# Making every second weight unit's low part by an accumulating DMA instead of a VectorE difference

## The chip, the cores and the metric

The kernel runs on one core of a Trainium2 chip. The metric is the device time of one execution in microseconds (us); the figure quoted is the median of several runs. The profile is one execution recorded by the hardware profiler.

## The reference, cut to what matters

Two layers of a hybrid backbone with 512 tokens (256 context, 256 latent) and 1024 channels in float32. In each layer a modulated RMS norm feeds one wide input projection; its columns go to three token mixers (a gated linear recurrence, a chunkwise retention with four heads, a latent attention with eight heads). Each mixer's output is gated, multiplied by a 1024x1024 down projection, weighted by a sigmoid merge gate and added; the sum goes through a 1024x1024 output projection and, gated, onto the residual.

```python
z = (m_a * ((ya * silu(ga)) @ w_down_a) + m_b * ((yb * silu(gb)) @ w_down_b)
     + m_c * ((yc * silu(gc)) @ w_down_c))
x = x + gate * (z @ w_out)
```

The second layer's output is wanted for the latent tokens only, so its queries, gates and down projections run on 256 columns, while its keys, values and recurrence inputs run on 512.

## The kernel before, in words

**Split operands.** TensorE works on `float32r` operands, which keep fewer bits than float32. To keep accuracy every operand is split into a high part (the value cast to `float32r`) and a low part (value minus high part, also `float32r`), and each product is three matmuls: high by high, high by low, low by high (`mm3`, line 520). `split` makes the pair: `A.copy(hi, src)` on ScalarE and `V.tensor_tensor(lo, src, f(hi), op=ALU.subtract)` on VectorE.

**Weight units.** The weights are packed into units of 128 partitions by 1024 floats (512 KB). There are 14 kinds of unit, eight of each kind (j = 0 to 7) and two layers: 224 units, fetched by `unit(l, kind, j)`. `load` takes a `raw` buffer, has SP's queue load the unit from HBM into it, takes one `whi` and one `wlo` buffer and splits `raw` into them. There are five buffers each of `raw`, `whi` and `wlo` (`NRAW`, `NHI`, `NLO`). The same `load` serves the smaller weights (`wup`, `wlru`, `wkv`, `wqd` and part of `wmod`), 72 more loads that are split. A unit feeds 24 matmuls of 512 columns, or of 256 columns in most of the second layer; an output unit (`wo`) there feeds twelve of 512.

**Who uses a unit.** `proj` multiplies one unit's eight 128x128 blocks with the normed tokens: inputs of the recurrence (`xa`), of the retention (`q`, `k`; values by `ret_pair`), the gates (`silu_gate`) and the merge gates. `merge` alternates, for j = 0 to 7, a merge gate unit and a down projection unit of the same j. The end of each layer takes the eight `wo` units: the first four for the left half of the columns, the last four, loaded together, for the right half; then come the residual and, in the second layer, the store of the output.

**The order of the work.** Nothing is emitted directly. A `Recorder` notes every operation with its buffers, and `schedule` replays the list in a planner: each operation has a cost from `_cost` (and for a DMA a lag to landing), engines take the earliest recorded operation that is ready and whose output buffer is free, and the resulting order is emitted engine by engine. So every engine runs a fixed order that depends on the planner's prices, and a changed price or operation can move all that comes after it. All recorded operations are emitted by one line, L368 of the profile. SP's price for a load is its bytes by 370 per ns plus 30 ns, with 2000 ns of lag; GpSimd ("POOL") so far does `power` (the norms' inverse square roots) and four small fills.

**Buffers.** A `raw` buffer is free for the next load when the high and low parts of its unit are made; `whi` and `wlo` are free when TensorE has run the unit's last matmul.

Of the kernel before, what the change touches and what calls it, by code (L numbers as in the profile page):

```python
# [12 lines left out]
F32R = mybir.dt.float32r  # L13
AF = mybir.ActivationFunctionType
ALU = mybir.AluOpType
# [30 lines left out]
UNIT = {kind: 8 * i for i, kind in enumerate(UNIT_KINDS)}  # L46
# [342 lines left out]
class Engine:  # L389
# [3 lines left out]
    def __getattr__(self, method):  # L393
        def call(*args, **kwargs):
            views = [x for x in list(args) + list(kwargs.values()) if isinstance(x, View)]
            outs = [x for x in (args[0], kwargs.get("accum_out")) if isinstance(x, View)]
            ins = [v for v in views if all(v is not o for o in outs)]
            cost, lag = _cost(self.name, method, args, kwargs)
            return self.rec.add(self.name, method, args, kwargs, outs, ins, cost, lag)

        return call
# [6 lines left out]
def _size(v):  # L408
    return v.idx.size


def _cost(engine, method, args, kwargs):
    out = args[0]
    n = _size(out) if isinstance(out, View) else 0
    if engine == "PE":
        if method == "transpose":
            return 107.0, 0.0
        passes = 1 if args[1].buf.dtype == F32R else 4
        return max(passes * n / 2.4, 27.0 if passes == 1 else 211.0) + 2.7, 0.0
    if engine == "SP":  # L420
        size = 4 * int(np.prod(args[1].shape))
        return size / 370.0 + 30.0, 2000.0
    psum = any(isinstance(x, View) and x.buf.psum for x in args[1:])
    if engine == "ACT":
        ptr = sum(isinstance(kwargs.get(k), View) for k in ("scale", "bias"))
        return (50.0 if psum else 93.0) + 0.834 * n + 93.0 * (ptr + ("accum_out" in kwargs)), 0.0
    if engine == "POOL":
        if kwargs.get("op") == ALU.pow:
            return 300.0 + 165.0 * n, 0.0
        return 100.0 + 2.2 * n, 0.0  # L430
    ptr = any(isinstance(x, View) for x in args[2:4])
    if method == "tensor_scalar":
        if psum:
            return 186.0 + 1.04 * n, 0.0
        return (129.0 if ptr else 67.0) + 0.523 * n, 0.0
    if method == "scalar_tensor_tensor":
        return 66.0 + (61.0 if isinstance(args[2], View) else 0.0) + 1.047 * n, 0.0
    if method in ("tensor_reduce", "bn_stats"):
        return 66.0 + 1.04 * _size(args[1]), 0.0
    if method == "reciprocal":  # L440
        return 66.0 + 6.3 * n, 0.0
    if method in ("tensor_copy", "memset"):
        return 66.0 + 0.53 * n, 0.0
    return 66.0 + 1.045 * n, 0.0
# [3 lines left out]
def tile_hybrid(ctx, tc, ins, out):  # L448
    nc = tc.nc
    rec = Recorder(nc)  # L450
    T, V, A, G, S = (Engine(rec, e) for e in ("PE", "DVE", "ACT", "POOL", "SP"))
# [51 lines left out]
    def f(ap):  # L503
        return ap.bitcast(F32)

    def split(hi, lo, src):
        A.copy(hi, src)
        V.tensor_tensor(lo, src, f(hi), op=ALU.subtract)
# [18 lines left out]
    def load_raw(src, n=1024):  # L527
        raw = rec.tile("raw", [128, 1024], F32)
        S.dma_start(raw[:, 0:n], src)
        return raw[:, 0:n]  # L530

    def load(src, n=1024):
        raw = load_raw(src, n)
        hi = rec.tile("whi", [128, 1024], F32R)[:, 0:n]
        lo = rec.tile("wlo", [128, 1024], F32R)[:, 0:n]
        split(hi, lo, raw)
        return hi, lo

    def unit(l, kind, j):
        return load(ins["wu"][l, UNIT[kind] + j])  # L540

    ident = ctile([128, 128], name="ident")
    make_identity(nc, ident.buf.tile())
# [136 lines left out]
    def proj(ps, l, kind, j, lat):  # L680
        hh, hl = hcur
        hi, lo = unit(l, kind, j)
        c = slice(256, 512) if lat else slice(0, 512)
        ps = ps[:, 0:256] if lat else ps
        mm3(ps, [(hi[:, k * 128:(k + 1) * 128], lo[:, k * 128:(k + 1) * 128], hh[:, k, c], hl[:, k, c]) for k in range(8)])
        return ps
# [274 lines left out]
    def merge(l, br, zt, first, last):  # L961
        names = {0: ("gmc", "dc"), 1: ("gma", "da"), 2: ("gmb", "db")}[br]
        n = 512 if l == 0 else 256
        slab = Slab()
        ys = ys_out[br]
        for j in range(8):
            pg = proj(bank(), l, names[0], j, l == 1)
            t = small()[:, 0:n]
            A.activation(t, pg, AF.Tanh, scale=0.5)
            yield  # L970
            hi, lo = unit(l, names[1], j)
            pd = bank()[:, 0:n]
            mm3(pd, [(hi[:, k * 128:(k + 1) * 128], lo[:, k * 128:(k + 1) * 128], *ys[k]) for k in range(8)])
            z = zt[j]
            if first:
                V.scalar_tensor_tensor(z, t, 1.0, pd, op0=ALU.add, op1=ALU.mult)
            else:
                V.scalar_tensor_tensor(t, t, 1.0, pd, op0=ALU.add, op1=ALU.mult)
                V.tensor_tensor(z, z, t, op=ALU.add)
            if last:  # L980
                zh, zl = slab.pair(n)
                A.activation(zh, z, AF.Copy, scale=0.5)
                V.scalar_tensor_tensor(zl, z, 0.5, f(zh), op0=ALU.mult, op1=ALU.subtract)
                zs.append((zh, zl))
            yield
# [18 lines left out]
    def ret_pair(l, p):  # L1004
        hh, hl = hcur
        banks = [bank() for _ in range(NTT)]
        for kp in range(4):
            hi, lo = unit(l, "v", 4 * p + kp)
            for tt in range(NTT):
                s = slice(tt * 128, (tt + 1) * 128)  # L1010
                for kk in range(2):
                    k = 2 * kp + kk
                    w = slice(kk * 512, (kk + 1) * 512)
                    mm3(banks[tt], [(hh[:, k, s], hl[:, k, s], hi[:, w], lo[:, w])], start=k == 0, stop=k == 7)
            yield
        vt = []
        for tt in range(NTT):
            vt.append(Slab().pair(512))
            split(*vt[-1], banks[tt])
        for i in range(2):  # L1020
            yield from ret_head(l, 2 * p + i, [(a[:, i * 256:(i + 1) * 256], b[:, i * 256:(i + 1) * 256]) for a, b in vt])
# [164 lines left out]
    for l in range(DEPTH):  # L1186
# [57 lines left out]
        for k2 in range(4):  # L1244
            hi, lo = unit(l, "wo", k2)
# [132 lines left out]
```

## Time and profile before

| what | value |
|---|---|
| device time, median of 3 runs | 1411.13 us (1410.71 to 1414.93) |
| profiled execution, first to last instruction (span) | 1409.4 us; no time of its own beside the span is recorded |
| TensorE (PE) busy | 1392.1 us, 99% |
| VectorE (DVE) busy | 1039.0 us, 74% |
| ScalarE (ACT) busy | 813.1 us, 58% |
| GpSimd (POOL) busy | 86.2 us, 6% |
| mean granted TensorE clock | 0.997 of full speed |
| DMA from HBM | 167.87 MB, 120 GB/s over the span |

"Busy" is the time in which an engine had at least one instruction running; durations of matmuls overlap, so their sum is more than the busy time. The DMA share is the mean busy share of the core's 16 DMA engines. "Landing" is the time from a DMA's issue to the arrival of its data.

### The profile page before, as it was taken

Reading aid. Unit: us, or ns where it says so; the run is one execution under the profiler, and the core shown is the slowest. Engines: PE = TensorE matmul, PEld = TensorE weight load, DVE = VectorE, ACT = ScalarE, POOL = GpSimd, SP = SyncE. Lnnn points to the kernel's source line nnn. Section 1 sums busy time; section 2 is a strip of 40 time slices with the busy share of each in tenths; the row PEclk is TensorE's granted clock in tenths of the full one; section 3 lists DMA queues with packets and bytes.
Section 4 is the critical chain, followed back from the end, with each engine's and each line's share of the span. In section 5 each row is a group of like instructions: output and inputs, shape, how many; then the busy total and the mean of one; then the engine's idle time right before and its main releaser. Section 6 shows DMA issues by size and latency. Waiting matters only on the chain.

```text
span 1409.4 us, 20895 instructions
## 1 busy us (share of the span) xinstructions
PE 1392.1 (99%) x7742; PEld 1211.3 (86%) x7742; DVE 1039.0 (74%) x2059; ACT 813.1 (58%) x1610; POOL 86.2 (6%) x112
## 2 busy tenths in 40 slices
PE   6999999999999999999999999999999999999998
PEld 3888888888888888888888888999898989899997
DVE  7689987667668655574884765899777888888664
ACT  7685664676668323153432226877686777854442
POOL 1031210000000000010000001311000000000000
PEclk9999999999999999999999999999999999999999
DMA  8512212223233423413344451332343444456452
GB/s 317 182 33 92 69 34 80 96 78 111 90 113 120 150 94 100 133 56 112 110 142 137 135 183 60 118 104 83 100 140 112 143 128 145 162 167 209 140 180 76
DMA packets 50990, 170.28 MB, mean 121 GB/s; under 512 B 5956, under 2 KB 7748, under 8 KB 50888
## 3 DMA queue, kind: packets, MB, share of 16 engines
q1 hardware_dynamic: 50888, 168.94, 36.0%
q8 instruction: 61, 1.00, 0.3%
q14 instruction: 41, 0.34, 0.1%
HBM read 167.87 MB, written 1.05 MB: 120 GB/s over the span
## 4 chain that ended last, share of the span: by engine, by line
PE 94%; DVE 3%; DMA 1%; ACT 1%; issue 0%; POOL 0%; SPq 0%; ACTq 0%; DVEq 0%; POOLq 0%
PE mm L368 94%; DVE sm L368 1%; DVE t L368 1%; DMA raw<-in_wmod_dram 1%; DVE wlo L368 1%; DMA t<-in_xin_dram 0%; DVE st L368 0%; POOL st L368 0%; ACT sm L368 0%; SPq L368 0%; ACT whi L368 0%; ACT t L368 0%; ACT hh L368 0%; DVE hl L368 0%; ACTq L368 0%
## 5 line engine op out<-in xcount | busy, mean ns | idle before, releaser
L368 ACT CAST whi<-raw 128x1024 fp32r<-128x1024 f32 (+3 forms) x296 | 292.3, 997 | 356.2 <-PE mm L368 292.0
L368 DVE TENSOR_TENSOR wlo<-raw,whi 128x1024 fp32r<-128x1024 f32 (+3 forms) x296 | 338.1, 1147 | 145.0 <-ACT whi L368 141.9
L368 PE MATMUL mm<-hh,whi 128*128 128x512 f32 (+1 forms) x1152 | 404.3, 351 | 0.0
L368 PE MATMUL mm<-hl,whi 128*128 128x512 f32 (+1 forms) x1152 | 402.6, 350 | 0.0
L368 PE MATMUL mm<-hh,wlo 128*128 128x512 f32 (+1 forms) x1152 | 402.6, 349 | 0.0
L368 PEld LDWEIGHTS mm<-hh,wlo 128*128 128x128 f32 x1152 | 218.0, 189 | 27.0
L368 PEld LDWEIGHTS mm<-hl,whi 128*128 128x128 f32 x1152 | 218.1, 189 | 26.4
L368 PEld LDWEIGHTS mm<-hh,whi 128*128 128x128 f32 x1152 | 218.0, 189 | 26.2
L368 PE MATMUL mm<-t,whi 128*128 128x512 f32 (+1 forms) x896 | 230.1, 344 | 0.0
L368 PEld LDWEIGHTS mm<-t,whi 128*128 128x128 f32 x896 | 156.0, 190 | 19.9
L368 POOL TENSOR_TENSOR st<-st,nhalf 128x2 f32<-128x2 f32 (+2 forms) x102 | 83.6, 826 | 1234.1 <-DVE st L368 1215.7
L368 PE MATMUL mm<-t,t 128*128 128x256 f32 (+1 forms) x912 | 153.6, 310 | 0.5 <-ACT t L368 0.5
L368 PE MATMUL mm<-t,wlo 128*128 128x512 f32 (+1 forms) x448 | 154.1, 344 | 0.0
L368 PE MATMUL mm<-whi,t 128*128 128x512 f32 (+1 forms) x464 | 146.0, 380 | 0.4 <-DVE t L368 0.4
L368 PEld LDWEIGHTS mm<-t,t 128*128 128x128 f32 x912 | 129.0, 190 | 11.0 <-ACT t L368 0.9
L368 ACT ACTIVATE sm<-mm 128x128 f32<-128x128 f32 (+4 forms) x278 | 95.4, 358 | 20.2 <-PE mm L368 17.1
L368 ACT CAST t<-sm 128x256 fp32r<-128x256 f32 (+1 forms) x128 | 60.6, 486 | 71.3 <-DVE sm L368 68.0
L368 PEld LDWEIGHTS mm<-whi,t 128*128 128x128 f32 x464 | 85.7, 188 | 11.7 <-DVE t L368 0.6
L368 PEld LDWEIGHTS mm<-t,wlo 128*128 128x128 f32 x448 | 84.9, 189 | 10.0
L368 PE MATMUL mm<-wlo,t 128*128 128x512 f32 (+1 forms) x232 | 88.0, 379 | 0.0
L368 PE MATMUL mm<-wlo,hh 128*128 128x512 f32 (+2 forms) x240 | 86.6, 363 | 0.0
L368 PE MATMUL mm<-whi,hh 128*128 128x512 f32 (+2 forms) x240 | 86.1, 362 | 0.4 <-ACT whi L368 0.4
(110 smaller groups left out, 1730.4 us busy)
## 6 DMA issues: line engine op xcount, KB each, us to landing
raw<-in_wu_dram SPq DMA_DIRECT2D x224, 512.0 KB, 3.5
raw<-in_wmod_dram SPq DMA_DIRECT2D x48, 512.0 KB, 4.5
t<-in_xin_dram SPq DMA_DIRECT2D x8, 512.0 KB, 7.5
raw<-in_wup_dram SPq DMA_DIRECT2D x8, 512.0 KB, 4.2
raw<-in_wlru_dram SPq DMA_DIRECT2D x16, 256.0 KB, 2.7
raw<-in_wqd_dram SPq DMA_DIRECT2D x8, 384.0 KB, 3.0
raw<-in_wup_dram SPq DMA_DIRECT2D x8, 384.0 KB, 3.1
raw<-in_wkv_dram SPq DMA_DIRECT2D x8, 320.0 KB, 3.9
```

The lines of the kernel that those rows point to most:

```text
L368: getattr(eng[op.engine], op.method)(*[r(x) for x in op.args], **{k: r(v) for k, v in op.kwargs.items()})
```

## The change

The planner gets a price for a DMA issued by GpSimd, and every unit with an odd j goes through a new `load_summed`: the cast into `whi` stays; ScalarE also writes minus the high part into `wlo`; then a DMA issued by GpSimd adds the raw weights onto it, both ends in SBUF.

```diff
     if engine == "POOL":
+        if method == "dma_start":
+            return 1100.0, 4000.0
         if kwargs.get("op") == ALU.pow:
@@
+    def load_summed(src):
+        raw = load_raw(src)
+        hi = rec.tile("whi", [128, 1024], F32R)
+        lo = rec.tile("wlo", [128, 1024], F32R)
+        A.copy(hi, raw)
+        A.activation(lo, f(hi), AF.Copy, scale=-1.0)
+        G.dma_start(lo, raw, accum_op=ALU.add)
+        return hi, lo
+
     def unit(l, kind, j):
-        return load(ins["wu"][l, UNIT[kind] + j])
+        return (load_summed if j % 2 else load)(ins["wu"][l, UNIT[kind] + j])
```

## Rows read from the trace of the kernel before

**Rows 1.** The page's part 1: busy time, share of span and instructions by engine.

```profile
PE 1392.1 (99%) x7742; PEld 1211.3 (86%) x7742; DVE 1039.0 (74%) x2059; ACT 813.1 (58%) x1610; POOL 86.2 (6%) x112
```

**Rows 2.** Windows of 35 us, all engines: busy us (instructions), then TensorE clock, DMA share, GB/s.

```profile
0.00:35.00 35.00, 24.22 (x110) 12.50 (x111) 24.70 (x43) 26.45 (x39) 4.81 (x14) 0.95 0.87 317
35.00:70.00 35.00, 33.97 (x202) 31.10 (x200) 23.76 (x56) 23.98 (x59) 2.76 (x4) 0.95 0.57 186
70.00:105.00 35.00, 34.47 (x196) 30.12 (x195) 28.46 (x94) 29.97 (x120) 12.10 (x16) 1.00 0.11 33
105.00:140.00 35.00, 34.48 (x199) 29.32 (x198) 33.80 (x116) 20.62 (x74) 6.74 (x6) 1.00 0.29 93
245.00:280.00 35.00, 35.00 (x156) 28.96 (x156) 22.84 (x29) 22.38 (x30) 0.00 (x0) 1.00 0.30 97
```

**Rows 3.** The page's part 4: the chain of waits, shares by engine.

```profile
PE 94%; DVE 3%; DMA 1%; ACT 1%; issue 0%; POOL 0%; SPq 0%; ACTq 0%; DVEq 0%; POOLq 0%
```

**Rows 4.** Groups of instructions over the span, costliest first: ScalarE, VectorE, GpSimd.

```profile
L368 ACT CAST whi<-raw 128x1024 fp32r<-128x1024 f32 (+3 forms) x296 | 292.3, 997 | 356.2 <-PE mm L368 292.0 <-issue 42.1 <-DMA raw<-in_wu_dram 13.6
L368 DVE TENSOR_TENSOR wlo<-raw,whi 128x1024 fp32r<-128x1024 f32 (+3 forms) x296 | 338.1, 1147 | 145.0 <-ACT whi L368 141.9
L368 POOL TENSOR_TENSOR st<-st,nhalf 128x2 f32<-128x2 f32 (+2 forms) x102 | 83.6, 826 | 1234.1 <-DVE st L368 1215.7 <-ACT t L368 12.0 <-DVE sm L368 5.4
```

**Rows 5.** Waits over the span, engines and the SP queue: us, times, longest.

```profile
ACT whi L368 <- PE mm L368: 292.0, 137, 4.9
...
SPq L368 <- DVE wlo L368: 923.8, 227, 20.9
```

**Rows 6.** DMA: two issue rows, SP's time per issue (ns), landing times of `raw` (us).

```profile
raw<-in_wu_dram SPq DMA_DIRECT2D x224, 512.0 KB, 3.5
raw<-in_wlru_dram SPq DMA_DIRECT2D x16, 256.0 KB, 2.7
...
L368 SPq DMA_DIRECT2D raw<-in_wu_dram x224: 327/328/328, 63.0 to 1379.7; - x112
DMA to landing us min/median/max: 2.4/3.5/9.3
```

**Rows 7.** Windows by stage of the second layer, all engines, columns as in Rows 2.

```profile
1085.00:1225.00 140.00, 140.00 (x923) 128.92 (x922) 119.59 (x207) 114.91 (x170) 2.62 (x4) 1.00 0.41 134
1225.00:1260.00 35.00, 35.00 (x224) 31.83 (x223) 29.89 (x48) 20.96 (x28) 0.00 (x0) 1.00 0.62 210
...
1330.00:1365.00 35.00, 35.00 (x292) 34.92 (x291) 22.20 (x32) 16.56 (x24) 0.00 (x0) 1.00 0.55 181
1365.00:1386.00 21.00, 21.00 (x165) 20.49 (x165) 13.62 (x20) 9.86 (x14) 0.00 (x0) 1.00 0.46 153
```

**Rows 8.** The same windows, VectorE's differences into `wlo` alone: window length, busy (count), clock, DMA, GB/s.

```profile
1085.00:1225.00 140.00, 42.35 (x38) 1.00 0.41 134
1225.00:1260.00 35.00, 12.59 (x12) 1.00 0.62 210
...
1330.00:1365.00 35.00, 14.66 (x13) 1.00 0.55 181
1365.00:1386.00 21.00, 8.89 (x8) 1.00 0.46 153
```

**Rows 9.** Timeline of the last stage, ScalarE and TensorE: start us, duration us.

```profile
1357.25 1.05 ACT L368 CAST whi<-raw 128x1024 fp32r<-128x1024 f32 x1 [1.40 <-PE mm L368]
1360.13 1.05 ACT L368 CAST whi<-raw 128x1024 fp32r<-128x1024 f32 x1 [1.55 <-issue]
...
1391.48 1.05 ACT L368 CAST whi<-raw 128x1024 fp32r<-128x1024 f32 x1 [1.67 <-PE mm L368]
...
1398.26 0.39 PE L368 MATMUL mm<-wlo,t 128*128 128x512 f32 x1
1404.61 0.39 PE L368 MATMUL mm<-whi,t 128*128 128x512 f32 x1
```

## The prediction, made before the changed kernel ran

> **What bounds the kernel now.** I read the busy times first, then the windows, the chain, the groups with their waits, the DMA and at last the timeline. TensorE is busy for 1392.1 of 1409.4 us, VectorE for 74% and ScalarE for 58% of the span [rows 1]. Of TensorE's 17.3 us of idle time 10.8 lie in the first 35 us and 2.1 between 35 and 140 us; a window in the middle of the first layer shows 35.00 of 35.00 [rows 2]; the rest, 4.4 us, is the span after the last matmul, which ends at 1405.0 us [rows 9]. The chain agrees: 94% of it is matmuls, 3% VectorE [rows 3]. So work taken off VectorE is worth nothing unless TensorE waited for it, and the first load of a unit that could change starts only at 63 us [rows 6]. What can change the time is a low part that comes too late.
>
> How early they come now is seen in the waits: ScalarE's cast waited 292.0 us for TensorE to leave a `whi` buffer, and SP's loads 923.8 us for VectorE to finish with a `raw` buffer [rows 5]. Buffers are kept full; loads run as soon as a buffer is given back.
>
> **The change part by part.** Of each kind's eight units four have an odd j: 14 x 4 x 2 = 112 units.
>
> *VectorE loses* 112 differences of 1.15 us [rows 4], 128 us, from 74% to about 65%. They lay beside matmuls, so this gives 0; at most the 2.1 us of idle TensorE time between 35 and 140 us come back.
>
> *ScalarE gains* 112 copies of 128x1024. I price each as the cast of that size, 1.05 us [rows 9]: 118 us, from 58% to 66%. The tightest stage is 1085 to 1225 us, where it is busy 114.9 of 140 us [rows 7]; 38 split units run there [rows 8], so about 19 copies add 20 us: 134.9 of 140. It still fits: 0, with a rival below.
>
> *GpSimd gains* 112 issues beside 102 powers of 0.83 us [rows 4]. The trace has no DMA of GpSimd. SP's issue takes 0.33 us [rows 6], the planner's new price in the diff is 1.1; I take 1.1, with 0.33 and 2.2 as ends. That makes 123 us on an engine busy for 86. A power queued behind such an issue waits for the copy before it plus 1.1 us; the powers stand mostly where norms are made, with few units about, so 0, at most 1 us.
>
> *The low part comes later.* Before, 1.05 us of cast and 1.15 of difference lay between a free buffer and a finished unit. After, it is cast, copy and X, from the issue of the adding DMA to its landing. Bounds for X from loads: the shortest landing is 2.4 us; the longest, 9.3, plus once more the transfer and 1.1 of issue gives 12.0 [rows 6]. In between, 256 KB land in 2.7 us and 512 KB in 3.5 [rows 6]: 1.6 us per 512 KB moved and 1.9 fixed. The add has two inputs of 512 KB, so I take X = 1.1 + 1.9 + 2 x 1.6 = 6.2 us.
>
> TensorE needs a refilled buffer only after the four other units. Casts of successive units in the last merge stand 2.88 us apart (1357.25, 1360.13) [rows 9], so the lead there is 4 x 2.88 = 11.5 us, against 1.05 + 1.05 + 6.2 = 8.3. Hidden, with 3.2 us left. In the first layer 156 matmuls take 35 us [rows 2], 5.4 us per unit of 24, and the lead is 21.5 us: hidden even at X = 12.0. At that end 2.6 us would be missing in the second layer, once per eight units or so (a stall gives the next units their lead back). On SP, `raw` is held for 8.3 us in place of 2.2, and all loads queue behind the one that waits for it; with 3.5 us for the next load that is 11.8 us, under the five units' 14.4. Hidden too, at this X.
>
> *The end* has no such lead. The last unit's cast starts at 1391.48, when TensorE leaves a buffer, and its low part is first used at 1398.26 [rows 9]. The new chain is ready at 1391.48 + 2.1 + 6.2 = 1399.8: **1.5 us late**, with everything after it. Ends: 0 (X under 4.7) and 5.8 us (X = 12.0).
>
> *The DMA engines gain* 112 transfers. The share of 0.55 at 181 GB/s between 1330 and 1365 us [rows 7] means 0.55 x 0.524 MB / 181 GB/s = 1.59 us of all 16 engines per 512 KB load. For the add I bound the engines' time c by 1.59 us (one move) and 4.8 us (two inputs and one output as three moves) and take two moves, 3.2 us, one per input, the middle of the two. That these transfers use the same 16 engines as the loads no row shows, since all data goes through one queue. I take it so; with engines of their own the terms that follow would be 0 and the sum 1.5 us. The Trainium skill, DMA: Bandwidth & Descriptors, section Issuing engines are not separate DMA queues, says that DMAs of SP, ScalarE and GpSimd end on the same 16 engines and interleave; no run here shows it yet, and by it the terms stand.
>
> Now by stage, loads plus adds [rows 7, 8]. 1085 to 1225 us: 0.41 x 140 + 19 x 3.2 = 118 of 140 us, fits. 1225 to 1260: 0.62 x 35 + 6 x 3.2 = 40.8 of 35, **5.8 us short**. 1330 to 1386: 0.55 x 35 + 0.46 x 21 + 10.5 x 3.2 = 62.3 of 56, **6.3 us short**. The 3.2 us of lead left take up a part of each: 2.6 + 3.1 = 5.7 us of waiting matmuls. The middle of the first layer, 0.30 x 35 + 3.25 x 3.2 = 21 of 35 [rows 2], fits.
>
> **Sum:** 0 + 0 + 0 + 5.7 + 1.5 = 7.2 us on the span of 1409.4, so 1416.6. The runs' median of 1411.13 is 1.7 us above that span, which I carry over: **1418.3 us**, 0.5% slower. About 0.3%, 4.2 us, is what a measurement of this kernel can tell from no change.
>
> **Rival 1, not slower: the add is cheap.** Both inputs lie in SBUF and the loads' rate is one from HBM; nothing says that an SBUF read takes as long. At c = 2.4 the two short stages need 36.1 of 35 and 54.1 of 56 us, which the lead covers, X becomes 5.4 and the end 0.7 us late: 1411.13 + 0.7 = 1411.8. It decides below c = 3.0, where the three terms together fall under 4.2 us. For it: 3.0 is near what I take. Against it: the adding DMA does more per byte than a load. The Trainium skill, DMA: Bandwidth & Descriptors, section Where 436 GB/s comes from, has transfers inside SBUF bound by a fabric of 435 GB/s; two inputs would then take 2.4 us, an estimate from that page, and the sum would be this rival's. No run here shows that rate.
>
> **Rival 2, much slower: the add is heavy.** At three moves, c = 4.8, the stage from 1085 needs 148 of 140, that from 1225 50.5 of 35, the last 79 of 56: 46 us short, less 3.2 in each of the three, and X = 7.8 puts the end 3.1 us late: about 40 us, 1451. For it: the same arithmetic with one move more. Against it: the planner's price of a load, by its formula 3.4 us, is close to the 3.5 that the trace shows [rows 6], and its new price of an add is 5.1 us in all, less than even my X.
>
> **Rival 3, slower by a little: ScalarE's order.** In 1085 to 1225 us 25.1 us are free for 19 copies; above 1.32 us per copy, its own and what its waits add, ScalarE is the bound and casts come late. At some 5 us of lost time: 1416. For it: the chance waits of a full engine. Against it: the lead of 11.5 us and more.
>
> **Faster** would need TensorE's idle time; 2.1 us are to be had, 1409.0, not measurable. Only a luckier order of the planner could give more.
>
> **How the numbers follow.** Forecast 0.38 (its own range, c from 3.0 to 3.5, 1415 to 1424; at its low edge 0.05 of it is no measurable change), rival 1 0.37, rival 2 0.12, rival 3 0.08, a luckier order 0.05. Slower: 0.33 + 0.12 + 0.08 = 0.53; same: 0.37 + 0.05 = 0.42; faster 0.05. The range starts at 1409, rival 1 with the early idle time back, and ends at 1447, where most of rival 2 and the luckier order are left out, under 2 in 10; it holds the case of X = 12.0 without short DMA engines (four stalls of 2.6 us for the 33 units of the last three windows [rows 8] and 5.8 us at the end: 1427).
>
> **What would show it.** Right: 112 fewer VectorE differences and 112 more ScalarE copies; TensorE still at 35.00 of 35.00 in windows of the first layer; its first waits for a DMA into `wlo` between 1225 and 1260 us and after 1330, some 3 us each, with DMA shares near 1; one wait of about 1.5 us before the last `wo` unit. Wrong: a DMA share well below 0.9 there (rival 1), waits from 1085 us on or in the first layer (rival 2), TensorE waiting for casts while ScalarE is busy (rival 3), waits of norms for GpSimd, or a granted clock below 1.00 after 70 us, which I don't expect.

## The result, and the profile after

The changed kernel takes **1422.92 us** (median of 4 runs, 1421.28 to 1423.40) against 1411.12 us before in the same session: a ratio of 1.0080, with a 95% interval from 1.0068 to 1.0092. It is 11.8 us slower; the forecast was 7.2 us, 1418.3. The profiled execution took 1423.4 us, 1421.6 of them its span. One execution among all the runs below, of the kernel with the add's traffic but without its waits, stood at a granted clock of 0.753 (1725.7 us) and is in no figure here.

The page of the kernel after: busy time by engine, the DMA queues, the chain, two groups of part 5 and three rows of DMA issues (KB each, median us from issue to landing).

```profile
PE 1395.7 (98%) x7742; PEld 1211.2 (85%) x7742; DVE 918.4 (65%) x1947; ACT 919.6 (65%) x1722; POOL 182.4 (13%) x224
...
q1 hardware_dynamic: 50888, 168.94, 35.6%
q0 software_dynamic: 16128, 58.73, 22.3%
...
PE 88%; DMA 5%; issue 3%; ACT 3%; DVE 2%; POOL 0%; SPq 0%; POOLq 0%; DVEq 0%; ACTq 0%
...
L368 POOL DMA_DIRECT2D wlo<-raw x112 | 97.4, 870 | 932.9 <-ACT wlo L368 710.9
...
L368 ACT ACTIVATE wlo<-whi 128x1024 fp32r<-128x1024 f32 x112 | 118.3, 1058 | 1.0
...
raw<-in_wu_dram SPq DMA_DIRECT2D x224, 512.0 KB, 4.1
wlo<-raw POOLq DMA_DIRECT2D x112, 512.0 KB, 5.1
raw<-in_wmod_dram SPq DMA_DIRECT2D x48, 512.0 KB, 5.1
```

The change does what it says: 112 VectorE instructions fewer, 112 ScalarE copies and 112 GpSimd DMAs more. VectorE is relieved by 120.6 us [rows 1], and the kernel is slower. DMA has gone from 1% to 5% of the chain, while TensorE fell from 94% to 88% [rows 3]. The loads of `wu` land after 4.1 us instead of 3.5 [rows 6], those of `wmod`, the modulation's weights, after 5.1 (4.5 before).

Where TensorE lost its time is seen in the windows (columns as in [rows 2]: TensorE, weight loads, VectorE, ScalarE, GpSimd; granted clock, DMA share, GB/s).

```profile
35.00:70.00 35.00, 33.25 (x198) 30.99 (x198) 23.80 (x56) 24.06 (x60) 2.74 (x4) 0.95 0.57 178
...
105.00:140.00 35.00, 34.02 (x199) 29.67 (x198) 32.71 (x118) 22.73 (x79) 7.59 (x8) 1.00 0.47 123
245.00:280.00 35.00, 35.00 (x156) 29.00 (x155) 19.91 (x27) 25.14 (x33) 2.77 (x4) 1.00 0.62 158
...
1085.00:1120.00 35.00, 34.23 (x248) 32.19 (x247) 26.65 (x52) 33.46 (x49) 4.82 (x5) 1.00 0.50 128
1120.00:1155.00 35.00, 34.21 (x195) 30.04 (x195) 23.22 (x42) 29.23 (x42) 4.30 (x5) 1.00 0.87 233
1155.00:1190.00 35.00, 35.00 (x257) 33.29 (x256) 22.42 (x47) 29.66 (x43) 4.54 (x6) 1.00 0.55 145
1190.00:1225.00 35.00, 32.71 (x198) 28.39 (x198) 25.06 (x42) 31.80 (x45) 2.58 (x3) 1.00 0.77 215
1225.00:1260.00 35.00, 31.68 (x186) 28.11 (x186) 23.42 (x40) 25.29 (x32) 4.30 (x5) 0.95 0.84 232
...
1295.00:1330.00 35.00, 34.53 (x244) 32.27 (x242) 22.49 (x45) 18.66 (x28) 3.44 (x4) 1.00 0.90 252
1330.00:1365.00 35.00, 35.00 (x293) 34.92 (x292) 15.53 (x32) 21.63 (x31) 6.32 (x8) 1.00 0.88 229
1365.00:1400.00 35.00, 35.00 (x275) 34.16 (x275) 14.29 (x24) 22.97 (x30) 5.16 (x6) 1.00 0.98 275
```

TensorE is idle for 25.9 us of the span instead of 17.3, 8.6 more. Of these 7.6 lie between 1085 and 1330 us, the input projections, recurrence, retention and first merges of the second layer, where it lost nothing before [rows 7]: 0.77 + 0.79 + 2.29 + 3.32 + 0.47. Nearly all of the rest lies before 140 us. The other 3.6 us of the longer span are not idle time: TensorE is busy for 1395.7 us instead of 1392.1 with as many matmuls. In the stage from 1085 to 1330 us two things make busy time longer. A mean clock of 0.95 in 1225 to 1260 us costs 0.05 x 35 = 1.8 us there (the kernel before had such a stretch in its first 35 us [rows 2], which the kernel after hasn't). And part of each wait counts as busy: matmuls of 512 columns start 0.23 us apart but are recorded as 0.39 us long (1244.81 and 1245.04 in the timeline below), so the first 0.16 us of a wait for the next one can't be seen as idle. GpSimd's powers, the same in both kernels, give the delay as a running sum: the one at 1098.6 us before comes 0.5 us earlier, that at 1171.56 comes 2.4 us later (1173.97), that at 1276.21 11.2 later (1287.38) and that at 1319.86 11.3 later (1331.15). So some 11.7 of the span's 12.2 us, idle time and slower matmuls together, are lost between 1098 and 1276 us of the old time.

After 1330 us TensorE is at 35.00 of 35.00, with the DMA engines busy for 0.88 and 0.98 of the time: the forecast's place for most of the loss (3.1 us of DMA engines and 1.5 of the end) is full, and TensorE doesn't wait there.

The waits of the kernel after (engine and line, what it waited for, us in total, times, longest): first the engines and SP's queue over the span, then TensorE from 60 us on.

```profile
DVE t L368 <- DMA raw<-in_wmod_dram: 22.9, 11, 5.8
...
SPq L368 <- DMA wlo<-raw: 635.1, 109, 15.3
SPq L368 <- DVE wlo L368: 443.5, 116, 20.9
...
PE mm L368 <- ACT t L368: 6.4, 5, 3.3
...
PE mm L368 <- DMA wlo<-raw: 0.8, 1, 0.8
```

TensorE hardly waits for a low part made by a DMA: 0.8 us, once. It waits for ScalarE's casts of activations. Further up, VectorE waits for loads of `wmod` 22.9 us, 11 times (3.3 us, 4 times before), and SP's queue waits for the adds where before it waited mostly for VectorE [rows 5]. The timeline of the largest gap shows how these hang together (start, duration, idle time before it and its releaser in brackets).

```profile
1233.02 1.81 POOL L368 DMA_DIRECT2D wlo<-raw  x2 [18.22 <-ACT wlo L368]
...
1238.45 0.33 SPq L368 DMA_DIRECT2D raw<-in_wmod_dram  x1
...
1246.17 0.75 DVE L368 SCALAR_TENSOR_TENSOR t<-raw,cf,t 128x512 f32<-128x512 f32 x1 [2.21 <-DMA raw<-in_wmod_dram]
...
1247.84 0.42 DVE L368 TENSOR_TENSOR sm<-sm,t 128x256 f32<-128x256 f32 x1
...
1248.29 0.40 ACT L368 CAST t<-sm 128x256 fp32r<-128x256 f32 x1 [3.85 <-DVE sm L368]
...
1244.81 0.39 PE L368 MATMUL mm<-whi,hl 128*128 128x512 f32 x1
1245.04 0.39 PE L368 MATMUL mm<-whi,hh 128*128 128x512 f32 x1
1248.75 0.54 PE L368 MATMUL mm<-t,whi 128*128 128x256 f32 x1 [3.32 <-ACT t L368]
1249.08 0.63 PE L368 MATMUL mm<-wlo,hh 128*128 128x512 f32 x1
```

Read it from the top. GpSimd issues an add at 1233.02; only when it has landed, 5.4 us later, is `raw` free, and SP can load the next piece of `wmod`, at 1238.45 (SP's queue waits for adds five times between 1220 and 1262 us, 23.6 us in all). That load takes 7.7 us, to 1246.17, while the DMA engines are busy with adds and loads. VectorE's multiply for the second layer's modulation (`mod_gates`) has stood waiting for it, and behind it in VectorE's fixed order stands a sum of the retention (1247.84) that has nothing to do with `wmod`. ScalarE stands 3.85 us for that sum, and TensorE 3.32 us for ScalarE's cast. Then matmuls take 0.63 us in place of 0.39, at the lower clock (0.50 of full speed, 1.2 GHz, from 1250 to 1252 us):

```profile
1250.00:1252.00 2.00, 2.00 (x7) 1.69 (x6) 1.90 (x5) 2.00 (x3) 0.86 (x1) 0.50 0.44 166
```

The stretch from 1190 to 1225 us lost its 2.3 us in another way, through ScalarE.

```profile
1186.77 0.33 SPq L368 DMA_DIRECT2D raw<-in_wlru_dram  x1
...
1193.78 0.62 ACT L368 CAST whi<-raw 128x512 fp32r<-128x512 f32 x1 [2.47 <-DMA raw<-in_wlru_dram]
...
1196.93 1.54 PE L368 MATMUL mm<-t,whi 128*128 128x512 f32 x6 [0.94 <-ACT t L368]
1212.14 0.74 PE L368 MATMUL mm<-t,whi 128*128 128x512 f32 x2 [0.96 <-ACT t L368]
```

A load of `wlru`, again behind an add, takes 7 us; ScalarE's cast of it waits 2.47 us. From there to 1213 us ScalarE pauses once, for 0.23 us: casts, copies and activations stand one behind the other, and TensorE waits for two of its casts, 0.94 and 0.96 us. Here a late load meets an engine that has no pause in which to catch up; three of the new copies run between 1190 and 1214 us.

### The profile page after: what moved, and what is told of

Its sections match the earlier page's. It is cut to its first block, busy times and chain, and to the rows that moved or that the text cites. A ratio compares the mean times of both kernels' runs of the same rounds, so it can differ in the third digit from the quotient of the medians.

```text
span 1421.6 us, 21264 instructions
## 1 busy us (share of the span) xinstructions
PE 1395.7 (98%) x7742; PEld 1211.2 (85%) x7742; DVE 918.4 (65%) x1947; ACT 919.6 (65%) x1722; POOL 182.4 (13%) x224
## 3 DMA queue, kind: packets, MB, share of 16 engines
q0 software_dynamic: 16128, 58.73, 22.3%
HBM read 167.87 MB, written 1.05 MB: 119 GB/s over the span
## 4 chain that ended last, share of the span: by engine, by line
PE 88%; DMA 5%; issue 3%; ACT 3%; DVE 2%; POOL 0%; SPq 0%; POOLq 0%; DVEq 0%; ACTq 0%
PE mm L368 88%; DMA raw<-in_wmod_dram 2%; DMA wlo<-raw 1%; ACT t L368 1%; DVE t L368 1%; ACT whi L368 1%; DMA raw<-in_wlru_dram 0%; DMA t<-in_xin_dram 0%; DVE sm L368 0%; ACT sm L368 0%; DMA raw<-in_wu_dram 0%; POOL st L368 0%; DVE wlo L368 0%; ACT L368 0%; DVE st L368 0%
## 5 line engine op out<-in xcount | busy, mean ns | idle before, releaser
L368 DVE TENSOR_TENSOR wlo<-raw,whi 128x1024 fp32r<-128x1024 f32 (+4 forms) x184 | 202.3, 1104 | 83.8 <-ACT whi L368 80.2
L368 POOL DMA_DIRECT2D wlo<-raw x112 | 97.4, 870 | 932.9 <-ACT wlo L368 710.9
L368 PEld LDWEIGHTS mm<-t,t 128*128 128x128 f32 x912 | 129.1, 190 | 11.2 <-ACT t L368 1.2
L368 ACT ACTIVATE wlo<-whi 128x1024 fp32r<-128x1024 f32 x112 | 118.3, 1058 | 1.0
L368 ACT ACTIVATE sm<-mm 128x128 f32<-128x128 f32 (+4 forms) x278 | 95.3, 360 | 17.9 <-PE mm L368 17.3
L368 DVE SCALAR_TENSOR_TENSOR sm<-sm,mm 128x512 f32<-128x512 f32 (+1 forms) x80 | 43.9, 549 | 88.5 <-PE mm L368 69.8
L368 PEld LDWEIGHTS mm<-whi,t 128*128 128x128 f32 x464 | 85.7, 188 | 11.9 <-DVE t L368 0.6
L368 PEld LDWEIGHTS mm<-t,wlo 128*128 128x128 f32 x448 | 85.0, 190 | 11.2 <-DVE wlo L368 1.0
```

The costliest lines, as they stand in the source:

```text
L368: getattr(eng[op.engine], op.method)(*[r(x) for x in op.args], **{k: r(v) for k, v in op.kwargs.items()})
```

## The experiments

All edits are shown against the kernel after, unless the kernel before is named. The first two ask for the place of the loss.

**Sums in the first layer only.**

```diff
-        return (load_summed if j % 2 else load)(ins["wu"][l, UNIT[kind] + j])
+        return (load_summed if j % 2 and l == 0 else load)(ins["wu"][l, UNIT[kind] + j])
```

> The change made in the first layer only (56 of the 112 units). In the trace of the changed kernel all of the lost time lies between about 1100 and 1280 us, in the second layer. All three theories (T1: raw buffers come back late and loads with them; T2: ScalarE's added copies; T3: the adds slow the loads on the shared DMA engines) expect 1410 to 1413 us. If it is 1417 or more, the place is wrong: the first layer's reordering costs something that shows only later.

Measured: 1410.81 us against 1411.12 (1.0001, 0.9992 to 1.0010). Half of all the adds cost nothing that can be measured.

**Sums in the first layer and, in the second, in the last merges, the last gates and `wo` alone.**

```diff
-        return (load_summed if j % 2 else load)(ins["wu"][l, UNIT[kind] + j])
+        return (load_summed if j % 2 and (l == 0 or kind in ("gmb", "db", "wo", "gc")) else load)(ins["wu"][l, UNIT[kind] + j])
```

> The change in the first layer and, of the second, only in the gates of the attention, the last merge and the output projection (kinds gc, gmb, db, wo); the units of the crowded middle of the second layer (recurrence, retention, the first two merges) are made as before. The theory of place, that the loss is made in that middle, expects 1410 to 1414 us. The prediction's terms (DMA engines short after 1330 us, the last unit late) would still cost here: 1415 to 1418.

Measured: 1411.02 us against 1410.99 (1.0001, 0.9992 to 1.0010). Its windows, without and with the sums:

```profile
1225.00:1260.00 35.00, 35.00 (x220) 31.67 (x219) 29.90 (x48) 20.02 (x28) 0.00 (x0) 1.00 0.62 204
...
1330.00:1365.00 35.00, 35.00 (x292) 34.92 (x292) 14.91 (x24) 22.32 (x31) 5.23 (x6) 1.00 0.91 246
```

The last merge runs here with the DMA engines at 0.91, where they stood at 0.55 before [rows 7], and TensorE loses nothing in it or at the end of the kernel. So the two terms that the forecast had after 1330 us are zero, and the 11.8 us come only with the 40 units of the other ten kinds in the second layer.

**Four raw buffers instead of five, in the kernel before.** A buffer that is held longer is like one buffer fewer.

```diff
-NRAW = 5
+NRAW = 4
```

> The kernel before with four raw buffers in place of five: no adds, no copies, only less time between a buffer's return and the next need of it. T1 expects a loss like the change's in the same stretch, 1415 to 1425. T2 and T3 expect 1410 to 1413.

Measured: 1413.39 us (1.0015, 1.0005 to 1.0024), and TensorE at 35.00 of 35.00 in each window from 1085 us on. T1 had expected 1415 to 1425: fewer buffers alone don't reproduce the loss.

**The copies without the adds: ScalarE writes minus the high part, VectorE then overwrites it with the difference.**

```diff
-        G.dma_start(lo, raw, accum_op=ALU.add)
+        V.tensor_tensor(lo, raw, f(hi), op=ALU.subtract)
```

> The kernel before plus the 112 copies on ScalarE (each overwritten by VectorE's difference, which stays); no adding DMA. T2 expects 1417 to 1423. T1 and T3 expect 1410 to 1413: raw is held only about 1 us longer than before and the DMA engines carry loads alone.

Measured: 1414.14 us (1.0023, 1.0013 to 1.0033), 3.0 us slower. Its one lossy window of the stage shows ScalarE at 32.37 of 35 us:

```profile
1190.00:1225.00 35.00, 33.66 (x198) 29.00 (x197) 31.64 (x49) 32.37 (x46) 0.00 (x0) 1.00 0.53 174
```

That lies between the two ranges expected. ScalarE's load and the new order cost 1.3 us in this window and 3.0 over the run, a quarter of the loss; the rest comes with the adds.

**The copy on VectorE instead of ScalarE.**

```diff
-        A.activation(lo, f(hi), AF.Copy, scale=-1.0)
+        V.tensor_scalar(lo, f(hi), -1.0, None, op0=ALU.mult)
```

> The changed kernel with the copy of minus the high part made by VectorE in place of ScalarE; the adding DMA stays. T2 (ScalarE's 112 copies) expects most of the 11.8 us back: 1411 to 1415. T1 and T3 (late raw buffers, slower loads) expect 1419 to 1425, since raw is held as long and the DMA engines move as much.

Measured: 1427.33 us (1.0120, 1.0105 to 1.0135). That is outside both ranges. GpSimd's powers are late by 3.4 us at 527, 8.4 at 854, 12.4 at 1098 and 14.8 at 1276: most of the loss lies ahead of the stage in question, where a new order of the engines moves the time by as much as the change does. In the stage itself only 2.4 us are lost where the change lost 11.7, and TensorE is idle for 2.4 us from 1085 to 1330 us instead of 7.6, though the adds are all there and take as long to land (6.5 us in the median there, 6.6 in the change). So the adds with their traffic and their hold did not make the loss of that stage once ScalarE was relieved (27 to 28 of 35 us in each window from 1085 to 1225 us, instead of 29 to 33). Whether that is ScalarE's relief or the other order, this run doesn't tell.

**A planner that expects loads to be late.** The lag of a load goes from 2000 to 5000 ns; nothing else is touched.

```diff
-        return size / 370.0 + 30.0, 2000.0
+        return size / 370.0 + 30.0, 5000.0
```

> The changed kernel with the planner's lag of a load from HBM raised from 2.0 to 5.0 us; the work is the same, only the fixed orders of the engines differ. T3 (loads come later than the order allows for, and VectorE and ScalarE stand in order behind what waits for them) expects much of the loss back: 1411 to 1417. T2 (ScalarE's copies are simply too much work there) expects 1420 to 1425.

Measured: 1415.51 us (1.0038, 1.0025 to 1.0050), from 1414.04 to 1419.31: 7.4 us of 11.9 come back. VectorE's waits for `wmod` fall from 22.9 to 0.5 us. In its profiled execution (1419.04 us) the window of the largest gap is whole again, the one before it not:

```profile
1190.00:1225.00 35.00, 32.70 (x193) 28.62 (x192) 24.83 (x41) 30.41 (x43) 3.19 (x4) 0.95 0.80 220
1225.00:1260.00 35.00, 35.00 (x225) 31.87 (x224) 23.77 (x42) 27.97 (x38) 4.29 (x5) 1.00 0.85 225
```

The DMA share is what it was (0.85). What changed is the order in which the engines stand behind loads: traffic of that share need not stop TensorE there, while an order planned for an idle DMA let it.

**The second layer's gates without their `wmod` loads.** They read tokens already in SBUF instead, which leaves out the gates' values.

```diff
-            raw = load_raw(ins["wmod"][l, 4 * c + kp])
+            raw = load_raw(ins["wmod"][l, 4 * c + kp]) if l == 0 or c < 4 else f(hcur[0][:, 2 * kp:2 * kp + 2, :].rearrange("p k t -> p (k t)"))
```

> The changed kernel without the second layer's eight loads of modulation weights: its gate sums read the normed tokens that lie in SBUF in place of the loaded weights, so the gates' values are left out, with VectorE's work the same. T3 with these loads as the link expects 1412 to 1417, since the longest waits of VectorE in the stretch are for them. T2 expects 1420 to 1424. If it stays at 1420 or more, these waits only show a delay that something else makes.

Measured: 1417.28 us (1.0043, 1.0028 to 1.0058): 5.6 us come back, 0.3 us short of T3's range. Its window of the largest gap is whole, that before it isn't, and ScalarE is nearly full there:

```profile
1190.00:1225.00 35.00, 32.92 (x201) 28.61 (x200) 31.44 (x52) 32.45 (x46) 2.58 (x3) 1.00 0.74 205
1225.00:1260.00 35.00, 35.00 (x230) 32.11 (x229) 24.23 (x41) 28.55 (x37) 4.30 (x5) 1.00 0.77 199
```

So the gap of 3.3 us goes with these loads, as the chain over `wmod` would have it, though the order is new here too. The losses between 1085 and 1225 us have another link: as in the change, a late load of `wlru` (one cast waits 2.2 us for it in the window of 32.92) meets a ScalarE that is 93% busy.

**A small add, in the kernel before.** The new path runs for 32 of 1024 columns, 16 KB; VectorE makes the others as before.

```diff
+        A.copy(hi, raw)
+        A.activation(lo[:, 0:32], f(hi[:, 0:32]), AF.Copy, scale=-1.0)
+        G.dma_start(lo[:, 0:32], raw[:, 0:32], accum_op=ALU.add)
+        V.tensor_tensor(lo[:, 32:1024], raw[:, 32:1024], f(hi[:, 32:1024]), op=ALU.subtract)
```

> The kernel before with a small adding DMA in each odd unit: 32 of the 1024 columns are copied and added that way, the rest stays VectorE's difference. raw is held, and the low part is ready, only when the add has landed, but it moves 1/32 of the bytes and ScalarE's copies are short. T1 (late raw and late low parts by themselves) expects 1415 to 1423. T2 and T3 expect 1410 to 1413.

Measured: 1417.02 us (1.0043, 1.0028 to 1.0058). That is in T1's range and looks like half of the loss, but its place is another: between 105 and 140 us TensorE is busy for 31.29 of 35, against 34.48 before [rows 2], and from 1085 to 1330 us it loses 1.5 us in place of 7.6. The issue costs GpSimd 873 ns for 16 KB as for 512 KB, and the small add lands in 2.2 us:

```profile
DMA to landing us min/median/max: 2.0/2.2/6.2
```

**Full copies and the small add, in the kernel before.**

```diff
-        A.activation(lo[:, 0:32], f(hi[:, 0:32]), AF.Copy, scale=-1.0)
+        A.activation(lo, f(hi), AF.Copy, scale=-1.0)
```

(the edit is against the small add's kernel)

> ScalarE's full copies and an add by DMA of 32 columns only, the other 992 stay VectorE's difference (which overwrites the copy there): ScalarE as loaded as in the change, raw held until an add has landed, but 1/32 of the adds' traffic and VectorE not relieved. If full ScalarE and late raw buffers together make the loss, without the traffic: 1419 to 1425. If the traffic of the adds is needed: 1414 to 1418, about the sum of the two single losses (3 and 2 us in the stretch, with the 2 to 4 us outside it that the small adds showed).

Measured: 1412.34 us (1.0007, 0.9997 to 1.0016), no difference that can be told, and less than either range expected. All of the new instructions and waits are in it, all of ScalarE's load, and VectorE is not relieved; what is missing is the add's bytes and its time. It does more than the kernel of the small add and is 4.7 us faster, which again gives the size of what a new order does by itself. One small part of the loss needs no large add: from 1085 to 1120 us TensorE is idle for 0.92 us here and 1.05 with the small add, as in the change (0.77).

**The copy on GpSimd.**

```diff
-        A.activation(lo, f(hi), AF.Copy, scale=-1.0)
+        G.tensor_scalar(lo, f(hi), -1.0, None, op0=ALU.mult)
```

> The changed kernel with the copy of minus the high part made by GpSimd, ahead of its adding DMA; ScalarE has the work of the kernel before, VectorE is relieved as in the change, the DMA engines carry all of the adds. If the loss in the middle of the second layer needs ScalarE's copies as well as the adds (T2 with T3), it mostly goes: 1411 to 1415 us. If the adds with their traffic do it alone (T3), it stays: 1419 to 1425. Against both: GpSimd's copy is slower than ScalarE's, so low parts come later still.

Measured: 1443.45 us (1.0231, 1.0215 to 1.0246). The group of the copies on GpSimd:

```profile
L368 POOL TENSOR_SCALAR wlo<-whi 128x1024 fp32r<-128x1024 f32 x112 | 323.1, 2893 | 629.1 <-ACT whi L368 629.0
```

At 2.89 us a copy instead of 1.06 low parts come still later, and 7 us are lost by 854 us already. ScalarE's relief can't be told from that.

**The add's traffic without its waits, in the kernel before.** ScalarE's copies stay, VectorE makes the difference as before, and for each odd unit GpSimd adds 512 KB onto a scratch buffer that nobody reads.

```diff
+        A.copy(hi, raw)
+        A.activation(lo, f(hi), AF.Copy, scale=-1.0)
+        s = big(F32)
+        G.memset(s, 0.0)
+        G.dma_start(s, f(hcur[0][:, 0:2, :].rearrange("p k t -> p (k t)")), accum_op=ALU.add)
+        V.tensor_tensor(lo, raw, f(hi), op=ALU.subtract)
```

> ScalarE's copies, VectorE's difference kept, and for each odd unit an adding DMA of 512 KB within SBUF whose result nobody reads (normed tokens onto a zeroed spare buffer, zeroed by GpSimd): the adds' traffic and ScalarE's load as in the change, but no unit waits for an add and raw is given back as early as in the kernel before. If slower loads on the shared DMA engines make the loss (T3 with T2): 1419 to 1425. If the loss comes from the time for which raw and the low part wait for the add (T1 with T2): 1412 to 1416.

Measured: 1422.60, 1424.27 and 1426.65 us, a ratio of 1.0089 (1.0072 to 1.0106). The whole loss is there, though no `raw` buffer and no low part waits for an add. Where it lies no trace shows, and it can't be said to be the traffic alone: ScalarE has its copies, and the scratch buffer is one of those that hold activations, filled by GpSimd and held until the add has landed.

**A long hold without the traffic, in the kernel before.** Two small adds, one after the other, with VectorE's difference for the other 960 columns.

```diff
+        A.activation(lo, f(hi), AF.Copy, scale=-1.0)
+        G.dma_start(lo[:, 0:32], raw[:, 0:32], accum_op=ALU.add)
+        s = stat()
+        G.tensor_tensor(s, f(lo[:, 0:1]), nhalf[:, 0:1], op=ALU.mult)
+        G.dma_start(lo[:, 32:64], raw[:, 32:64], accum_op=ALU.add)
+        V.tensor_tensor(lo[:, 64:1024], raw[:, 64:1024], f(hi[:, 64:1024]), op=ALU.subtract)
```

> ScalarE's full copies and two small adds of 32 columns each, the second issued only when the first has landed; the other 960 columns stay VectorE's difference. raw and the low part wait about as long as in the change (two landings of some 2.2 us each and what lies between), with 1/16 of the adds' traffic. T1 with T2: 1417 to 1425. T3 with T2: 1411 to 1415, as with one small add.

Measured: 1416.75 us (1.0036, 1.0023 to 1.0048), between the two ranges. In the stage from 1085 to 1330 us a small add lands in 3.2 us (median) and a large one of the change in 6.6, so two in a row hold `raw` about as long. TensorE is idle for 1.4 us there:

```profile
1190.00:1225.00 35.00, 33.94 (x206) 29.54 (x205) 30.84 (x50) 32.67 (x48) 10.11 (x13) 1.00 0.56 169
...
1295.00:1330.00 35.00, 34.67 (x245) 32.43 (x244) 24.95 (x52) 18.30 (x28) 11.18 (x17) 1.00 0.59 172
```

The hold, with ScalarE's copies but without the bytes, doesn't make the losses of the stage; with the run before it this points to the bytes in flight, and the loads that they make late, as one thing that they need.

No version was faster than the kernel before. The two that keep their sums out of the second layer's middle equal it, and the one with full copies and small adds can't be told from it.

## Why the prediction was right, and where it was wrong

**Sign and size** came out: 1422.9 us lies inside the range and in the forecast's own range of 1415 to 1424. But the sum was right for terms that turned out to be zero, and the time was lost where I had written zero: that the number fits is luck. With the measured 2.83 us of the engines and 5.1 us of landing put into the forecast's own sum, the two stages are 3.7 and 2.6 us short, less than the 4.3 us of lead that would then be left (11.5 - 2.1 - 5.1), and the end is 0.4 us late: 1411.5 us, no change that can be told.

**VectorE, 0: right.** The groups show 112 differences of 128x1024 gone, at 1.22 us where I had taken the mean over all sizes, 1.15. The 120.6 us of busy time bought nothing.

**GpSimd, 0: right, its price too high.** An issue takes 0.87 us, not 1.1, and from 1085 to 1290 us VectorE waits for a power once, 0.7 us.

**X, 6.2 us: too high.** Issue to landing is 5.1 us (4.5 to 9.6) over the run. In the stage that lost the time it is 6.6, so there the estimate was a little low. TensorE's waits for `wlo` from a DMA come to 0.8 us, so the lead of the buffers nearly always covers the new low part, as argued.

**The end, 1.5 us: wrong, 0.** The forecast kept the order of the old timeline. The planner, which knows a price for the add, laid the last matmuls in another order, and TensorE runs through them:

```profile
1406.01 0.86 POOL L368 DMA_DIRECT2D wlo<-raw  x1 [4.58 <-ACT wlo L368]
...
1409.72 0.39 PE L368 MATMUL mm<-wlo,t 128*128 128x512 f32 x1
1410.62 0.39 PE L368 MATMUL mm<-wlo,t 128*128 128x512 f32 x1
...
1416.74 0.39 PE L368 MATMUL mm<-whi,t 128*128 128x512 f32 x1
```

The last add is issued at 1406.01; the matmuls with low parts go on at 0.68 us each, with one step of 0.90 us (1409.72 to 1410.62) that holds three matmuls with high parts instead of two. The last matmul ends 4.5 us before the span does, against 4.4 before [rows 9].

**The DMA engines, 5.7 us: 0 for what was meant.** The term's two parts were waits for low parts while the DMA engines are short. After 1330 us nothing is lost; between 1225 and 1260 us 3.3 us are, but through the chain over `wmod` and not for a low part. The step that failed is c, "take two moves, 3.2 us". The queue of the adds took 22.3% of 1421.6 us for 112 of them: 2.83 us of all 16 engines each. That is under the 3.0 at which the forecast itself turned to rival 1, and the last stage fills up without TensorE waiting (0.91 in the run with sums in the tail). That the adds use the loads' engines was right: the share rises to 0.98 and loads take longer. The Trainium skill, DMA: Bandwidth & Descriptors, section Issuing engines are not separate DMA queues, says the same, and this trace agrees. From the rate in its section Where 436 GB/s comes from the forecast had worked out 2.4 us; the measured 2.83 is above that estimate, and it decides.

**"`raw` is held for 8.3 us … Hidden too, at this X": the step that carried the loss.** The working there asked only whether the next *weight unit* comes in time, and it nearly does: from 60 us on TensorE waits 1.8 us for high and low parts (0.8 for one by a DMA, 0.8 for one by VectorE, 0.2 for a cast). But the five `raw` buffers and SP's queue also serve `wmod` and `wlru`, whose users have less lead: VectorE and ScalarE stand in a fixed order behind them, with the retention's and recurrence's work next in line. And I judged the stage from 1085 to 1225 us by the sum of its DMA time, "118 of 140 us, fits": the share in its windows is 0.50, 0.87, 0.55, 0.77, uneven, and loads come late in the full ones. The forecast named waits from 1085 us on as what would show it wrong, and they are there; they are not rival 2's, which needed a c of 4.8.

**ScalarE, 0, with rival 3 at 0.08: partly wrong.** The sum of 134.9 of 140 us wasn't reached: 124.2 in the four windows to 1225 us, with 15 of the 19 copies made by then. But a cast that meets a late load in an engine at 31.8 of 35 us has no room to catch up; TensorE's idle time is charged to casts (6.4 us). ScalarE's share alone is small (3.0 us in the run with copies only, 0.8 with copies and small adds). But the adds without its copies lost little in the stage too (2.4 us, in the run with the copy on VectorE): it is the two together that go with the loss, the late loads and an engine without slack. The forecast's sign of rival 3, TensorE waiting for casts while ScalarE is busy, is there from 1190 to 1225 us.

**Shown and open.** Shown by runs: the place (sums in the first layer and in the tail are free); that neither the copies, nor the hold, nor one buffer fewer makes the stage's losses by itself; that the gap of 3.3 us goes without the loads of `wmod` and with an order that expects late loads. In the stage from 1085 to 1330 us TensorE is idle for 1.3 us with the copies alone, 1.4 with copies and a long hold, 2.4 with the adds and ScalarE relieved, and 7.6 with all of it. Argued from this, and not shown: that copies and traffic must come together. Against it stands the copy on GpSimd, where ScalarE is relieved and the loss is larger, with low parts that come later. Read from one trace, and not tried by itself: the chains from an add over a late load to the cast. Open: how the 11.8 us divide among traffic, hold and ScalarE. Each edit lets the planner lay every order anew, which by itself moves the time by about 5 us (the two kernels with small adds differ by 4.7 us, the larger one faster), so the 7.4 and 5.6 us that came back are no exact shares.

## What to carry to other kernels

When work moves to a DMA, ask not only whether its own consumer can wait, but who else uses the buffer that it holds and the engines that it fills: here the users of side loads through the same pool, with less lead, were hit first, and the weight units hardly. An order fixed in advance from the latency of an idle DMA can break when traffic is added; planned with a lag of 5 us instead of 2 for a load, the same work gave 7.4 of the 11.8 us back. An engine without slack passes a late load on: here one was followed by two waits of nearly 1 us each. And relief of an engine for which the bound engine doesn't wait is worth nothing: 120.6 us of VectorE bought 0.

## What the runs showed of the hardware

An add from SBUF to SBUF of 512 KB took 2.83 us of the 16 DMA engines, 1.8 times the 1.59 us of a load, and 5.1 us from issue to landing; one of 16 KB still took 2.1 to 2.5 us (medians of three runs). GpSimd's issue of such a DMA cost 0.87 us at either size, against 0.33 for SP's issue of a load [rows 6]. Loads of weight units slowed from 3.5 to 4.1 us beside the adds. From 1085 to 1330 us the median of all loads into `raw` rose from 3.9 to 4.5 us and the longest from 7.0 to 9.0, and the adds themselves took 6.6. A copy of 128x1024 took 2.89 us on GpSimd, 1.06 on ScalarE and 0.69 on VectorE. And the granted clock, which I had expected at 1.00 after 70 us, fell to 0.50 (1.2 GHz in place of 2.4) behind the gap of 3.3 us without a matmul, and was 1.00 again from 1254 to 1256 us. Matmuls of 512 columns took 0.63 us instead of 0.39 meanwhile, so that this gap cost some 1.8 us more than its length.
